# Windowed attention on one core: two adjacent rows per partition, or two blocks of 128 rows, in one transfer

## The chip, the core and the metric

The kernel runs on one core of a Trainium2 chip. The metric is the device time of one execution, in microseconds. Inputs and output lie in HBM, in float32.

## The reference

Queries, keys and values are `[4, 4096, 1536]`. The sequence is cut into windows of 64 rows, and attention is computed inside each window alone, over the full width of 1536:

```
q_w, k_w, v_w = x.reshape(B, S // 64, 64, D)          # B 4, S 4096, D 1536
logits = einsum('bnwd,bnud->bnwu', q_w, k_w) * D**-0.5
attn   = softmax(logits, axis=-1)
out    = einsum('bnwu,bnud->bnwd', attn, v_w)
```

Over the four batches there are 16,384 rows. The three inputs are 302 MB and the output is 100.7 MB.

## The kernel before

The rows of all batches are one list. `plan` (L25) cuts it into units: 63 body units of 256 rows, then two tail units of 128 rows. A unit has `G` blocks, and in each block a partition holds `R` adjacent rows; a unit is `128 * G * R` rows. The body has `BODY_G, BODY_R = 1, 2` (L40), the tail has `G = R = 1`.

`dram(x, u)` (L74) gives the view of HBM for a transfer: partition p, block g, and then R rows in one run. With R = 2 a partition's run is two adjacent rows, 12 KB of float32.

`load(u)` (L80) issues three transfers on GpSimd's queue (POOL, q0), for q, k and v; each casts to fp16 on the way (L84). There are four buffers of each, and loads are issued `PREFETCH = 3` units ahead, at the head of a unit's turn. The framework gives eight completion semaphores in rotation to POOL's transfers, so a ninth waits until the one eight before it has landed.

`scores(u, g)` (L116) transposes q and k of a block on TensorE against an identity (L140), eight 128x128 pieces to a PSUM tile `tp`, and evicts each tile into `xt`, in turn on VectorE (L145) and ScalarE (L147). The scores are accumulated over 12 chunks of the width in `lt`. With R = 1 the matmuls of a chunk follow its eviction by one tile, through `mm` (L126); with R = 2 all of them come behind the last transposes, in `finish_scores` (L165), and there each of the two row slots of k meets both row slots of q, so that one matmul has 256 columns.

`finish_scores` (L155) then takes exp on ScalarE (L177) for the blocks of the same window alone, and writes it into `et`, a constant tile whose other places were set to zero once. A window is 32 partitions wide with R = 2 and 64 wide with R = 1, so four or two instructions.

`values` (L180) multiplies `et` by ones for the row sums (L187), takes reciprocals on VectorE (L192), and multiplies `et` by v in pieces of 512 columns (L198). With R = 2 each piece is the sum of two matmuls, one for each row slot of v. The results are scaled by the reciprocal on the way out of PSUM, the first and third piece on ScalarE (L204), the second on VectorE (L206).

The program order is written out by hand (`tc.manual_schedule()`). In each turn come the loads of the unit three ahead; then for each block its scores and the values of the block before it; and the store of a unit behind its last values. Stores are issued on SP's queue (q1, L216), those of the last body units and of the first tail unit on POOL's queue behind the last loads. The last unit is stored in three pieces of 512 columns from SP (L208).

Of the kernel before, what the change touches and what calls it, by code (L numbers as in the profile page):

```python
# [36 lines left out]
    return units  # L37


BODY_G, BODY_R = 1, 2  # L40
PREFETCH = 3


# [218 lines left out]
```

## Time and profile before

| | |
|---|---|
| median of 3 runs | 958.6 us (958.33 to 958.67) |
| the profiled execution, its time and its span | 958.6 us, 956.8 us |
| granted TensorE clock, mean | 0.88 |
| body load, KB written, median us from issue to landing | 768 KB, 38.0 to 40.4 |
| body store on SP's queue, KB, median us from issue to landing | 1536 KB, 11.4 |
| packets on q0 (loads, four stores), on q1 (other stores) | 28,656, 9,072 |

The span is what the profile covers, from the first instruction to the last. Loads are counted in the profile by the bytes they write, which with the cast are half of those read. A page shows the busy time of each engine, then the span in 40 slices with the busy tenths of each, then the DMA queues, the chain of work that ended last, and groups of instructions. Waits name the waiting instruction first and what released it behind the arrow; the numbers are the sum in us, how often, and the longest.

### The profile page before, as it was taken

The page shows a single profiled execution, that of the slowest core. Times are in us where ns is not written, and L with a number is a line of the kernel's source. Part 1 is how long each engine was busy: PE and PEld are TensorE (multiplying, and loading weights), DVE is VectorE, ACT ScalarE, POOL GpSimd, SP SyncE. Part 2 cuts the span into 40 slices and gives each one's busy share as a digit, 9 for nine tenths or more (in the row PEclk, how much of TensorE's full clock was granted, in tenths as well). Part 3 has the DMA queues.
Part 4 walks back from the last instruction along what each step waited for, and adds up shares of the span by engine and source line. Part 5 has one row for each costly group of instructions (what it writes and reads, how often), then busy time and mean ns, then how long its engine had stood idle before and what let it go on. Part 6 is the DMA issues. An engine that isn't in the chain of part 4 may idle for free.

```text
span 956.8 us, 13110 instructions
## 1 busy us (share of the span) xinstructions
PE 658.4 (69%) x5624; PEld 482.7 (50%) x5624; DVE 240.6 (25%) x392; ACT 456.1 (48%) x705; POOL 105.8 (11%) x204
## 2 busy tenths in 40 slices
PE   4776766767767677676776766767667667676674
PEld 3454554645545555455464554555545445445452
DVE  1222222222222222222222222222222222222222
ACT  2544545444445454454545544445445444454445
POOL 3111011110110111101111011011110111111000
PEclk9978889888898898888978989889988999898888
DMA  9999999999999999999999999999999999999996
GB/s 185 242 268 263 275 269 258 279 258 269 270 256 279 257 270 279 250 277 267 259 280 255 271 272 255 279 259 269 279 252 275 266 261 279 257 269 273 253 252 268
DMA packets 37786, 252.51 MB, mean 264 GB/s; under 512 B 4192, under 2 KB 4192, under 8 KB 29664
## 3 DMA queue, kind: packets, MB, share of 16 engines
q0 software_dynamic: 28656, 156.51, 78.0%
q1 hardware_dynamic: 9072, 95.16, 24.0%
q8 instruction: 44, 0.72, 0.3%
q14 instruction: 14, 0.11, 0.0%
HBM read 301.99 MB, written 100.66 MB: 421 GB/s over the span
## 4 chain that ended last, share of the span: by engine, by line
DMA 86%; PE 8%; ACT 4%; issue 1%; DVE 0%; POOL 0%; ACTq 0%; POOLq 0%; DVEq 0%
DMA k<-in_k_dram 40%; DMA v<-in_v_dram 40%; DMA q<-in_q_dram 6%; PE tp L140 3%; PE lt L165 3%; ACT xt L147 2%; PE o L198 2%; ACT et L177 1%; ACT out_sb L204 1%; DVE xt L145 0%; PE lt L126 0%; PE sp L187 0%; POOL q L84 0%; ACTq L257 0%; POOL v L84 0%
## 5 line engine op out<-in xcount | busy, mean ns | idle before, releaser
L140 PE MATMUL tp<-ident,k 128*128 128x128 f16 x1536 | 259.6, 270 | 172.9 <-DMA k<-in_k_dram 172.9
L147 ACT COPY xt<-tp 128x1024 f16<-128x1024 f16 x192 | 194.3, 1012 | 348.3 <-PE tp L140 348.3
L140 PE MATMUL tp<-ident,q 128*128 128x128 f16 x1536 | 253.6, 264 | 52.1 <-ACT xt L147 21.4
L140 PEld LDWEIGHTS <-k 128*128 128x128 f16 x1536 | 156.8, 125 | 184.0 <-DMA k<-in_k_dram 183.8
L198 PE MATMUL o<-v,et 128*128 128x512 f16 x762 | 185.1, 378 | 61.5 <-ACT out_sb L204 61.4
L145 DVE COPY xt<-tp 128x1024 f16<-128x1024 f16 x192 | 132.7, 691 | 346.5 <-PE tp L140 346.5
L140 PEld LDWEIGHTS <-q 128*128 128x128 f16 x1536 | 163.0, 120 | 97.3 <-issue 67.6
L165 PE MATMUL lt<-xt 128*128 128x256 f16 x1512 | 188.4, 277 | 0.5
L204 ACT ACTIVATE out_sb<-o,rs 128x512 f32<-128x512 f32 x256 | 168.9, 686 | 19.0 <-PE o L198 11.1
L165 PEld LDWEIGHTS <-xt 128*128 128x128 f16 x1512 | 144.6, 100 | 31.2 <-ACT xt L147 13.8
L177 ACT ACTIVATE et<-lt,zeros 32x128 f16<-32x128 f32 (+1 forms) x256 | 91.8, 358 | 124.5 <-PE sp L187 114.6
L198 PEld LDWEIGHTS <-et 128*128 128x128 f16 x762 | 69.0, 96 | 146.9 <-issue 79.2
L206 DVE TENSOR_SCALAR out_sb<-o,rs 128x512 f32<-128x512 f32 x128 | 96.1, 750 | 151.4 <-PE o L198 151.4
L84 POOL DMA_DIRECT2D v<-in_v_dram x65 | 34.4, 529 | 343.1 <-PE o L198 309.9
L84 POOL DMA_DIRECT2D k<-in_k_dram x65 | 34.5, 531 | 332.4 <-DMA v<-in_v_dram 332.4
L192 DVE RECIPROCAL rs<-sp 128x2 f32<-128x2 f32 (+1 forms) x65 | 11.1, 170 | 209.1 <-PE sp L187 209.1
L84 POOL DMA_DIRECT2D q<-in_q_dram x65 | 34.6, 532 | 141.6 <-DMA k<-in_k_dram 140.8
L187 PEld LDWEIGHTS <-et 128*128 128x128 f16 x254 | 15.7, 97 | 1.9 <-ACT et L177 0.5
L187 PE MATMUL sp<-ones,et 128*128 128x1 f16 x254 | 15.6, 164 | 0.1
L216 POOL DMA_DIRECT2D out_dram<-out_sb x4 | 2.1, 532 | 25.2 <-ACT out_sb L204 22.3
L126 PE MATMUL lt<-xt 128*128 128x128 f16 x24 | 2.4, 221 | 2.6 <-ACT xt L147 1.7
L126 PEld LDWEIGHTS <-xt 128*128 128x128 f16 x24 | 1.4, 98 | 3.3 <-ACT xt L147 2.0
(10 smaller groups left out, 3.0 us busy)
## 6 DMA issues: line engine op xcount, KB each, us to landing
out_dram<-out_sb SPq DMA_DIRECT2D x60, 1536.0 KB, 11.4
q<-in_q_dram POOLq DMA_DIRECT2D x63, 768.0 KB, 40.4
k<-in_k_dram POOLq DMA_DIRECT2D x63, 768.0 KB, 38.1
v<-in_v_dram POOLq DMA_DIRECT2D x63, 768.0 KB, 38.0
out_dram<-out_sb POOLq DMA_DIRECT2D x3, 1536.0 KB, 9.1
q<-in_q_dram POOLq DMA_DIRECT2D x2, 384.0 KB, 30.3
k<-in_k_dram POOLq DMA_DIRECT2D x2, 384.0 KB, 26.2
v<-in_v_dram POOLq DMA_DIRECT2D x2, 384.0 KB, 21.9
```

What stands on the lines that cost most here:

```text
L84: nc.gpsimd.dma_start(out=dst, in_=dram(src, u))
L126: nc.tensor.matmul(lv[:, r, :, :], lhsT=xt[:, c, 1, r, :], rhs=xt[:, c, 0, :R, :], start=(c == 0), stop=(c == DC - 1),)
L140: nc.tensor.transpose(tp[:, c - c0, x, r, :], src[:, g * R + r, c * P : (c + 1) * P], ident)
L145: nc.vector.tensor_copy(out=dst, in_=tp)
L147: nc.scalar.copy(out=dst, in_=tp)
L165: nc.tensor.matmul(lv[:, r, :, :], lhsT=xt[:, c, 1, r, :], rhs=xt[:, c, 0, :R, :], start=(c == 0), stop=(c == DC - 1),)
L177: nc.scalar.activation(et[s, :, :, s], lv[s, :, :, s], EXP, bias=zeros[s], scale=scale)
L187: nc.tensor.matmul(sp[:, t, 0:1], lhsT=et[:, r, t, :], rhs=ones[:, 0:1], start=(r == 0), stop=(r == R - 1),)
L192: nc.vector.reciprocal(out=rs, in_=sp[:, :, 0])
L198: nc.tensor.matmul(o, lhsT=et[:, r, t, :], rhs=u.v[:, g * R + r, sl], start=(r == 0), stop=(r == R - 1),)
L204: nc.scalar.activation(dst, o, COPY, bias=0.0, scale=rs[:, t : t + 1])
L206: nc.vector.tensor_scalar_mul(dst, o, scalar1=rs[:, t : t + 1])
```

## The change

One line differs:

```
-BODY_G, BODY_R = 1, 2
+BODY_G, BODY_R = 2, 1
```

A body unit is still 256 rows, loaded in three transfers and stored in one. Now it has two blocks of 128 rows, and a partition holds one row of each: rows p and p + 128 of the unit in place of rows 2p and 2p + 1. A partition's run in HBM is one row, 6 KB, and there are two of them in a transfer, 768 KB apart. On the chip the tiles keep their size.

Each block takes the path of R = 1 that the tail units already had: scores through `mm` with 128 columns behind the transposes of the tile before, a window of 64 partitions in two exps, one reciprocal, and one matmul for each piece of the values. The two blocks of a unit follow one another, each with the values of the block before it between. The transposes and evictions keep their number and their shapes. The `et` tile is 128x128 in place of 2x2 of these. The tail units, the queues, the buffers and the prefetch depth are as they were.

## The prediction

> **What bounds the kernel now.** I read the page from the top: the span, the slices, the DMA queues, the chain. The profiled execution took 958.6 us (span 956.8, 1.8 around it), which is also the median of the runs, so terms worked out from the trace are added to 958.6.
>
> ```profile
> span 956.8 us, 13110 instructions
> PE 658.4 (69%) x5624; PEld 482.7 (50%) x5624; DVE 240.6 (25%) x392; ACT 456.1 (48%) x705; POOL 105.8 (11%) x204
> ...
> DMA  9999999999999999999999999999999999999996
> ...
> q0 software_dynamic: 28656, 156.51, 78.0%
> q1 hardware_dynamic: 9072, 95.16, 24.0%
> ...
> HBM read 301.99 MB, written 100.66 MB: 421 GB/s over the span
> ...
> DMA 86%; PE 8%; ACT 4%; issue 1%; DVE 0%; POOL 0%; ACTq 0%; POOLq 0%; DVEq 0%
> ```
>
> No compute engine is over 69%, while the 16 DMA engines are full in 39 slices of 40 and their waits are 86% of the chain. The two queues' shares sum to over 100%: a packet's recorded time overlaps the next one's, so its time is not what it occupies. The queue counts tell the packets: 65 x 3 loads x 128 partitions are 24,960, the four q0 stores 512, and 199 DMAs x 16 completion packets 3,184, together the 28,656 of q0. So today one packet is one partition's contiguous run: 12 KB read (6 KB written as fp16) for a body load, 12 KB for a body store.
>
> The waits say whether the loads ever come too late to keep the DMA engines full:
>
> ```profile
> POOL k L84 <- DMA v<-in_v_dram: 332.4, 62, 6.4
> POOL v L84 <- PE o L198: 309.9, 57, 6.8
> ...
> PE tp L140 <- DMA k<-in_k_dram: 172.9, 63, 4.4
> ```
>
> POOL waits for an older load to land (eight are in flight, 38 to 40 us from issue to landing), and PE waits 2.7 us per unit for k. The queue never runs dry and compute has slack: PE's idle time in the body costs nothing.
>
> The price of a smaller packet stands in the trace itself, because the two tail units already use R=1: 6 KB read per packet. One stretch with body loads alone, one with tail loads alone:
>
> ```profile
> DMA packets 535, 2.97 MB, mean 212 GB/s; under 512 B 52, under 2 KB 52, under 8 KB 535
> q0 software_dynamic: 535, 2.97, 103.6%
> ```
> ```profile
> DMA packets 374, 1.05 MB, mean 210 GB/s; under 512 B 46, under 2 KB 46, under 8 KB 373
> q0 software_dynamic: 373, 1.03, 105.4%
> ```
>
> The first is 4 to 18 us, the second 925 to 930 us. Written rate 212 against 210 GB/s: the smaller packets lose about 1%, but a window only counts this to a few packets. The packet records behind these lines are finer. A 12 KB load packet takes 474 ns and the next on its engine starts 19 ns before it ends: 455 ns each. A 6 KB one takes 248 ns with the same 19 ns: 229 ns. Two make 458 to 459, so 3.5 ns is the cost of one more load packet.
>
> **The change, part by part.**
>
> Transfers: bytes, DMA count, order and queues stay. Each partition's 12 KB becomes two runs of 6 KB, 768 KB apart in HBM. Per DMA engine, body loads go from 63 x 3 x 8 = 1,512 packets to 3,024. Cost: 1,512 x 3.5 ns = 5.3 us, all on the path because the DMA engines are the bound.
>
> Stores: 60 body stores on SP's queue, 480 packets per engine, become 960. A 12 KB store packet takes 460 ns behind another store and 473 ns behind a load (88% of the 7,680 records), each with 4 ns of overlap: 456 or 469. The 6 KB store at the very end takes 234 ns, half of 460 plus 4. So two in a row cost 460 against 456, and two that each follow a load cost 2 x (234 + 13 - 4) = 486 against 469. Loads and stores now take turns packet by packet; I expect this to go on with twice as many turns: 480 x (0.88 x 17 + 0.12 x 4) = 7.4 us. If two packets of a store go in a row, it is 480 x 4 = 1.9 us. No row here shows a store of two runs per partition, so both ends are kept; I take 7.4, since in the trace the turns change after every packet. The three 1.5 MB stores on POOL add 24 packets, 0.1 us. Below nothing I exclude: a shorter packet never moved bytes faster in these records. The upper end for loads is that a load which takes turns with a store also pays 13 ns: 480 x 13 = 6.2 us more.
>
> Descriptors: POOL's instruction is 532 ns and twice the runs may make it or the start longer. First issue at 1.26 us, first packet at 2.63: at most 1.4 us of making them is exposed, once. Between 0 and 1.4 us; I take 0.5. Later it is hidden by seven other loads in flight: even at 2.8 us for each of 195 loads POOL would be busy 546 us of 958. SP's store instruction (332 ns) is hidden behind idle SP time; if its packets came slower, loads would fill the engines meanwhile.
>
> Compute: scores of a unit go from 24 matmuls of 256 columns (277 ns each) to 24 of 128 (221 ns), values from 12 of 512 columns to 6, row sums from 4 to 2, exps from four of 359 ns to four of 310, reciprocals from 1 to 2 (170 ns, on a DVE that is 25% busy); the 48 transposes and 6 evictions stay, in two groups of three with scores behind each. In the body all this lies beside the DMA: the chain from k's landing to the next unit takes 12.0 us (923.35 to 935.35) of a period of 14.7 (the last two body k land at 908.64 and 923.35), and falls to about 10.2 by the tail below. POOL's v load waits for PE's values of the unit before; these come earlier, after the first half of the unit's scores, so nothing behind it on POOL (the next q, k, v) is late. The new wait of q and k loads on PE is for a buffer whose transposes ended a unit earlier.
>
> The tail is where compute shows:
>
> ```profile
> 884.70 38.60 DMA k<-in_k_dram
> 923.35 1.69 PE tp L140 x14
> 929.82 1.70 PE lt L165 x14
> 940.12 1.47 PE o L198 x6
> 946.30 1.84 ACT out_sb L204 x3
> ```
>
> These are the longest pieces of the chain from 919 us. The last body unit's k lands at 923.3; from there PE and ACT set the pace to 948.1, then the last stores run to 953.1. A half unit with R=1 is like tail unit N-2: its scores took 3.3 us (935.35 to 938.7), the last values of the kernel 1.8 (946.3 to 948.1), so the last body unit takes 2 x 5.1 = 10.2 instead of 12.0, and the values of that unit in the next step 1.8 instead of 2.9. That is 2.9 us of chain. The stores left at that time can use only what the DMA engines were idle for, about 2.4 us between 941 and 949 by the packet records. Gain 2.4, at least 0.
>
> The sum: 958.6 + 5.3 + 7.4 + 0.1 + 0.5 - 2.4 = 969.5; I say 969.
>
> The Trainium skill, "DMA: Bandwidth & Descriptors", Specifications, says that a transfer of 512 B or more already runs at line rate. By that the smaller packets would cost nothing and only the tail would count, some 956 us. The records speak against it: 2 x 229 is more than 455. The same page, Why small descriptors are slow, gives a fixed overhead of about 3 cycles per packet; at the 850 MHz of its Specifications that is 3.5 ns, an estimate which the load records bear out, and for 1,512 + 504 packets it would make 7.1 us and a time near 963.8. It has nothing of the 13 ns that a store behind a load shows here, and there I follow the trace.
>
> **Rivals.**
>
> Stores go two in a row (chance 0.2). The engines' turn would then come after both runs of a partition. For it: nothing in the trace; against it: every packet boundary is a turn now. 958.6 + 5.3 + 1.9 + 0.1 + 0.5 - 2.4 = 964.0.
>
> Packet size costs nothing and the tail decides (0.1 for faster by over 0.2%, the bound of what a measurement of this kernel can tell from no change, 1.9 us). Mechanism: less matmul work after the last body k, in the 24.8 us chain at the end. Price: -2.4 to -2.9, so 955.7 to 956.2. For it: the rates 212 and 210 differ by little more than the count of a window allows. It decides if a doubled packet costs below 0.25 ns on average over the 2,016 added per engine (1,512 + 504; 0.5 us of the 2.4). Between that and 1.9 us slower the result would be no change (0.05).
>
> Each added packet costs all of its recorded fixed time (0.05). Doubling 248 and taking off 474 gives 22 ns; 2,016 x 22 = 44 us, with the tail about 1001. Against it: shares over 100% show that 19 of the 22 lie beside the next packet. Something in between, such as 6 KB pieces 768 KB apart reading slower than the tail's adjacent ones, is in this case too.
>
> The change does not do what it says: it does; the loads become 128 x 2 x 1536 and the descriptors cannot be merged, since the two runs are not adjacent in HBM.
>
> **How the numbers follow.** Turns packet by packet 0.6, two in a row 0.2, the full fixed time or slower reads 0.05: slower 0.85. Same 0.05, faster 0.1. The likeliest case alone spans 967 to 972. The range reaches down to two in a row with the larger tail gain, no start cost and loads at 3 ns (2 x 229 - 455), 964.0 - 0.5 - 0.5 - 0.8, about 962, and up to loads that pay for turns too, a late start and no tail gain: 969.5 + 6.2 + 0.9 + 2.4 = 979.
>
> **What would show it.** DMA slices still full; q0 near 28,656 + 24,192 + 384 = 53,232 packets and q1 near 16,752; in load-only windows about 210 GB/s written; store packets at 247 ns with loads between them (in a row: 234); PE's wait for k longer than 2.7 us per unit, its busy time down; the tail from the last body k to the last ACT about 22 us instead of 24.8. I am wrong if load packets no longer start 19 ns before the last one ends, if slices in the body fall below 9 (descriptors or buffers late), or if POOL's load instructions grow to several us.

## The result, and the profile after

The changed kernel takes 969.1 us (median of 4 runs, 968.98 to 969.20) against 958.6: a ratio of 1.011, 95% interval 1.0092 to 1.0127. It is slower, by 10.5 us, at the forecast 969. The sum met the time; one of its terms was right for the wrong reason, and the experiments show which. The profiled execution took 969.0 us.

The page of the changed kernel, with the span, the engines, the DMA slices and the queues (packets, MB, share of the 16 engines' span):

```profile
span 967.2 us, 12600 instructions
PE 497.1 (51%) x5120; PEld 369.4 (38%) x5120; DVE 250.5 (26%) x453; ACT 429.9 (44%) x705; POOL 141.5 (15%) x204
...
DMA  9999999999999999999999999999999999999998
...
q0 software_dynamic: 53232, 156.51, 80.5%
q1 hardware_dynamic: 16752, 95.16, 24.8%
...
HBM read 301.99 MB, written 100.66 MB: 416 GB/s over the span
```

TensorE lost 161 us of busy time, and the kernel became slower: the DMA engines are full as before and move the same bytes at 416 in place of 421 GB/s. The packet counts are those foretold. The granted TensorE clock fell from 0.88 to 0.79; e3 below, with this compute at a clock of 0.80, is not slower than the kernel before, so the clock is not what costs. The waits of the changed kernel (sum in us, times, longest):

```profile
PE tp L140 <- DMA k<-in_k_dram: 244.0, 63, 7.0
...
POOL k L84 <- DMA v<-in_v_dram: 187.7, 45, 6.9
```

PE's wait for k went from 2.7 to 3.9 us per unit, 71 us in all: part of the compute that was saved became waiting for loads. The stretch from 4 to 18 us, loads alone:

```profile
DMA packets 1013, 2.96 MB, mean 212 GB/s; under 512 B 48, under 2 KB 48, under 8 KB 1013
q0 software_dynamic: 1013, 2.96, 107.7%
```

Twice the packets, the same 212 GB/s to within what a window can count, and a share that rose from 103.6 to 107.7%: more of each packet's time lies over its neighbour's. The packet records have load packets at 248 ns with 19 ns of overlap (229 each) and store packets at 247 ns in 94% of 15,360 and 234 in the rest.

Two views bear on the start and on the end. POOL's load instructions for q (busy us, mean ns), first of the kernel before, then of the changed one:

```profile
L84 POOL DMA_DIRECT2D q<-in_q_dram x65 | 34.6, 532 | 141.6 <-DMA k<-in_k_dram 140.8
```
```profile
L84 POOL DMA_DIRECT2D q<-in_q_dram x65 | 46.2, 711 | 303.8 <-DMA k<-in_k_dram 297.9
```

and the closing waits on SP, first of the kernel before, then of the changed one:

```profile
SPq L257 <- PEq L257: 3.1, 2, 2.6
SPq L257 <- DMA out_dram<-out_sb: 3.0, 3, 1.9
```
```profile
SPq L257 <- DMA out_dram<-out_sb: 5.8, 3, 5.0
SPq L257 <- PEq L257: 1.0, 2, 0.5
```

Before, SP waited 1.9 us for the last stores and then 2.6 us for the other engines; after, 5.0 for the stores and 0.5 for the engines. The last store landed 12.5 us later (953.4 to 965.9), but the span grew by 10.4 only.

For the experiments I use one more number from the packet records: the time from the first packet to the last, less what the 16 engines were idle on average (an engine counts as idle for each packet under 16 that is in flight). It is 946.8 us before and 959.5 after, 12.7 more. Here I call it the transfer time.

### The profile page after: what moved, and what is told of

Same layout as the page of the kernel before. It is cut to its first block, busy times and chain, and to the rows that moved or that the text cites. A ratio compares the mean times of both kernels' runs of the same rounds, so it can differ in the third digit from the quotient of the medians.

```text
span 967.2 us, 12600 instructions
## 1 busy us (share of the span) xinstructions
PE 497.1 (51%) x5120; PEld 369.4 (38%) x5120; DVE 250.5 (26%) x453; ACT 429.9 (44%) x705; POOL 141.5 (15%) x204
## 5 line engine op out<-in xcount | busy, mean ns | idle before, releaser
L140 PEld LDWEIGHTS <-k 128*128 128x128 f16 x1536 | 176.2, 116 | 270.6 <-DMA k<-in_k_dram 261.5
L126 PE MATMUL lt<-xt 128*128 128x128 f16 x1536 | 178.2, 249 | 171.7 <-ACT xt L147 136.9
L140 PEld LDWEIGHTS <-q 128*128 128x128 f16 x1536 | 176.5, 115 | 72.7 <-DMA q<-in_q_dram 57.4
L126 PEld LDWEIGHTS <-xt 128*128 128x128 f16 x1536 | 109.6, 110 | 224.3 <-ACT xt L147 159.0
L177 ACT ACTIVATE et<-lt,zeros 64x64 f16<-64x64 f32 x256 | 79.2, 309 | 148.4 <-PE sp L187 143.6
L198 PE MATMUL o<-v,et 128*128 128x512 f16 x384 | 116.9, 417 | 0.5 <-ACT out_sb L204 0.5
L84 POOL DMA_DIRECT2D q<-in_q_dram x65 | 46.2, 711 | 303.8 <-DMA k<-in_k_dram 297.9
L192 DVE RECIPROCAL rs<-sp 128x1 f32<-128x1 f32 x128 | 21.5, 168 | 223.7 <-PE sp L187 223.7
L84 POOL DMA_DIRECT2D v<-in_v_dram x65 | 46.1, 709 | 211.4 <-DMA q<-in_q_dram 177.4
L198 PEld LDWEIGHTS <-et 128*128 128x128 f16 x384 | 30.9, 104 | 19.6 <-issue 7.0
L187 PEld LDWEIGHTS <-et 128*128 128x128 f16 x128 | 14.1, 110 | 0.6 <-ACT et L177 0.6
L216 POOL DMA_DIRECT2D out_dram<-out_sb x4 | 2.7, 679 | 22.1 <-ACT out_sb L204 18.8
```

The costliest lines, as they stand in the source:

```text
L84: nc.gpsimd.dma_start(out=dst, in_=dram(src, u))
L126: nc.tensor.matmul(lv[:, r, :, :], lhsT=xt[:, c, 1, r, :], rhs=xt[:, c, 0, :R, :], start=(c == 0), stop=(c == DC - 1),)
L140: nc.tensor.transpose(tp[:, c - c0, x, r, :], src[:, g * R + r, c * P : (c + 1) * P], ident)
L177: nc.scalar.activation(et[s, :, :, s], lv[s, :, :, s], EXP, bias=zeros[s], scale=scale)
L187: nc.tensor.matmul(sp[:, t, 0:1], lhsT=et[:, r, t, :], rhs=ones[:, 0:1], start=(r == 0), stop=(r == R - 1),)
L192: nc.vector.reciprocal(out=rs, in_=sp[:, :, 0])
```

## The experiments

### Loads alone, stores alone, compute alone

Loads in two runs (e1), on the kernel before:

```
+    def rows_of(x, u):
+        return x[u.row0 : u.row0 + u.rows].rearrange("(a p) d -> p a d", p=P)
...
-            nc.gpsimd.dma_start(out=dst, in_=dram(src, u))
+            nc.gpsimd.dma_start(out=dst, in_=rows_of(src, u))     # dst is [P, 2, D]
```

> The kernel before (R = 2, its compute and its 12 KB stores) with only the body loads cut into two runs of 6 KB, rows p and p + 128 of the unit (so its windows hold other rows than the reference's). Theory (a load packet costs 3.5 ns beyond its bytes, a store packet pays 13 ns when it follows a load): 1,512 more load packets per engine are 5.3 us, the number of turns between loads and stores stays, a late start adds 0.5: 964.4 us. Rival A (a packet costs its whole recorded fixed time, 22 ns): 1,512 x 22 = 33 us, 992. Rival B (packets are free, the slower time of the changed kernel comes from its compute or its clock): 958.6.

Measured: 963.7 us (before in that call 958.9), ratio 1.0049 (1.0034 to 1.0064).

```profile
span 961.7 us, 13110 instructions
...
q0 software_dynamic: 52848, 156.51, 81.1%
q1 hardware_dynamic: 9072, 95.16, 24.0%
```

Transfer time 952.7, so 5.9 us for 1,512 packets per engine: 3.9 ns each. The number of turns did not quite stay: 450 store packets per engine follow a load in place of 425 (those that take 473 ns). At 13 ns that is 0.3 us, and without it a load packet costs 3.7 ns. Both rivals are out.

Stores in two runs (e2), the same view for `out` and L216:

> The kernel before with only the stores cut into two runs of 6 KB (output rows in another order than the reference's); loads stay at 12 KB. Theory (loads and stores take turns packet by packet): 7.4 us from SP's stores and 0.1 from POOL's: 966.1 us. Rival A (two packets of a store go in a row): 1.9 us, 960.6. Rival B (store packets are free): 958.6.

Measured: 965.0 us, ratio 1.0065 (1.0048 to 1.0082).

```profile
span 963.0 us, 13110 instructions
...
q0 software_dynamic: 29040, 156.51, 77.4%
q1 hardware_dynamic: 16752, 95.16, 24.9%
```

Transfer time 953.2, 6.4 us more, about 1 us under the sum, with 88% of the store packets at 247 ns. Loads and stores do take turns packet by packet; "two in a row" (960.6) is out.

The changed compute with 12 KB transfers (e3), on the changed kernel:

```
+    def run_of(x, u):
+        return x[u.row0 : u.row0 + u.rows].rearrange("(p a) d -> p (a d)", p=P)
...
-            nc.gpsimd.dma_start(out=dst, in_=dram(src, u))
+            nc.gpsimd.dma_start(out=dst, in_=run_of(src, u))      # stores likewise
```

> The changed kernel's compute (G = 2, R = 1) with the transfers of the kernel before: 12 KB per partition for loads and stores (rows 2p and 2p + 1 land in the two blocks, so its windows hold other rows than the reference's). Theory (the body is DMA, and the shorter chain behind the last body k brings the end forward): the last store is issued 2.9 us sooner; by the engines' idle time 2.4 can be had: 956.2 us, between 955.7 and 956.5. Rival A (the end hangs on transfers that are late for another reason, and the shorter chain brings nothing): 958.6.

Measured: 958.0 us, ratio 0.999 (0.998 to 0.9999).

```profile
span 955.9 us, 12600 instructions
PE 498.7 (52%) x5120; PEld 370.5 (39%) x5120; DVE 250.4 (26%) x453; ACT 429.7 (45%) x705; POOL 105.7 (11%) x204
```

The whole compute change, 160 us of TensorE, is worth 0.9 us, which the interval barely tells from nothing. That is not the 956.2 of the theory, and lies outside its 955.7 to 956.5. The chain did get shorter: the last scaling on ScalarE ended at 946.2 in place of 948.7, POOL issued its last store 3.0 us sooner. But the last store landed only 0.75 us sooner (952.7 against 953.4). In the kernel before the 16 completions of the last store lie 0.17 us apart; here 2.4 us. The first of them came 3.0 us sooner (950.3 against 953.3), the last 0.75: what the shorter chain gave, most DMA engines could use and the latest hardly.

The three parts add: 4.8 + 6.1 - 0.9 = 10.0, against 10.5 for the change.

### A larger dose of the load packets

The kernel before with loads in four runs of 3 KB (e4):

```
+    def halves_of(x, u):
+        flat = x[u.row0 : u.row0 + u.rows].rearrange("s d -> (s d)")
+        return flat.rearrange("(a p e) -> p a e", p=P, e=D // 2)
...
+                nc.gpsimd.dma_start(out=dst, in_=halves_of(src, u))   # body units alone
```

> The kernel before with the body loads cut into four runs of 3 KB, 384 KB apart (the inputs are shuffled within a unit, so its output is not the reference's). A dose of the same: theory (3.5 ns per load packet, whatever its size): 3 x 1,512 more packets are 15.9 us, a later start about 1: 975.5 us. Rival A (22 ns each): 100 us, 1058. Rival B (packets are free): 958.6. Rival C (shorter runs far apart also read slower in HBM): more than 980, and load packets that take longer than 113 + 22 = 135 ns.

Measured: 974.0 us, ratio 1.0156 (1.0141 to 1.0172).

```profile
span 971.5 us, 13110 instructions
...
q0 software_dynamic: 101232, 156.51, 87.2%
```

Load packets of 3 KB take 135 ns, as foretold, and the transfer time is 963.6: 16.8 us for 4,536 packets per engine, 3.7 ns each, or 3.6 without the 46 turns more per engine (0.6 us). From 12 KB to 3 KB, with runs 768 or 384 KB apart, the price goes by the packet. The packets' recorded time on q0 rises by some 100 us per engine (78.0% of 956.8 us to 87.2% of 971.5), which is the sum of Rival A, for a cost of 17: a queue's share cannot be read as time. The Trainium skill, "DMA: Bandwidth & Descriptors", Why small descriptors are slow, has about 3 cycles per packet (3.5 ns at the 850 MHz of its Specifications, an estimate); e1 and e4 bear that out with 3.7 and 3.6.

### Taking the turns away

Every body store on POOL's queue, behind the loads, in the kernel before (e5) and the changed one (e6):

```
-        eng = nc.gpsimd if i >= N - PREFETCH - 2 else nc.sync
+        eng = nc.gpsimd
```

> The kernel before with every body store issued on POOL's queue, so that loads and stores lie in one queue, a store's eight packets per engine behind one another, and no turns are taken. Theory (a store packet pays 13 ns when it follows a load packet of the other queue): 480 x 0.88 x 13 ns = 5.5 us less: 953.3 us, with store packets at 460 ns. Rival (the 13 ns belong to reads and writes being in flight together, or the loads behind a waiting store come late): 958.6 or slower, store packets still at 473 ns.

> The changed kernel with every body store on POOL's queue. Theory: 960 x 0.94 x 13 ns = 11.7 us less than 969.1: 957.4 us, store packets at 234 ns; what is left over e5 (953.3) is the bytes-free cost of 2,016 shorter packets, 5.3 + 1.9 us, less the shorter end. Rival (the turn is not what costs): 969.

Measured: e5 953.7 us, ratio 0.9947 (0.9929 to 0.9965); e6 959.3 us, ratio 1.0007 (0.9998 to 1.0017) to the kernel before. First e5, then e6:

```profile
span 951.9 us, 13105 instructions
...
q0 software_dynamic: 37296, 250.89, 101.9%
```
```profile
span 957.7 us, 12595 instructions
...
q0 software_dynamic: 69552, 250.89, 105.1%
```

With one queue, 87% of the 12 KB store packets take 460 ns, 93% of the 6 KB ones 234. Nearly all others take 13 ns more, 62 and 61 per engine: about one for each of the 63 stores on POOL's queue, the first of its packets, which comes behind a load of the same queue. So the 13 ns go with a store packet that follows a load, whichever queue the load is of. One queue makes such turns rare: 62 per engine in place of 425 in the kernel before, 61 in place of 904 in the changed one.

Transfer times are 942.4 and 949.2: 4.4 and 10.3 us less than with two queues. That is 12.1 ns for each of 363 turns, and 12.2 for each of 843. With most turns gone, what e6 is above e5 is 5.6 us, and 6.8 of transfer time, against 5.3 + 1.9 foretold for the shorter packets alone. The changed kernel is then level with the kernel before. e6 missed its 957.4 by 1.9 us: the 61 turns that stay are 0.8 of it, and 12.2 in place of 13 ns another 0.7.

### What holds the end

In the kernel before, the store of unit N-2 moved to SP's queue (e7), and the same in the changed kernel (e8):

```
+        eng = nc.gpsimd if N - PREFETCH - 2 <= i < N - 2 else nc.sync
```

> The kernel before with the store of the first tail unit (768 KB) on SP's queue in place of POOL's. In the profile of before POOL's closing drain ends 8.2 us behind its last issue, at 956.05, and 2.6 us after the last store has landed (953.4). Theory (the end hangs on POOL's drain, some 4 us behind the landing of POOL's last transfer): POOL's last transfer then is the store before (landed at 949.3, so drained by 953.3) and SP ends at 953.6: 2.3 us less, 956.3 us. Rival (the end hangs on the stores' landing alone): 958.6.

> The changed kernel with the first tail unit's store on SP's queue. In its profile POOL's drain ends at 966.45 and SP's last wait at 966.1, behind the last landing at 965.9. Theory (its end hangs on the last landing, which some DMA engines reach 2.9 us after the first, and no longer on the drain as in the kernel before): 0.3 us less, 968.8 us. Rival (the drain holds it as it held the kernel before): 2.6 us less, 966.5.

Measured: e7 956.0 us, ratio 0.9973 (0.9963 to 0.9983); e8 968.5, which is 9.7 us over the kernel before of its call, against 10.5. The closing waits on SP of e7:

```profile
SPq L257 <- DMA out_dram<-out_sb: 1.7, 3, 0.6
...
SPq L257 <- PEq L257: 0.7, 2, 0.5
```

The drain is the last long instruction on POOL, at L257; in the kernel before it starts at 947.8, takes 8.2 us (8217 ns) and ends at 956.05:

```profile
L257 POOLq DRAIN  x3: 46/102/8217, 947.8 to 956.6; - x3
```

In e7 the 2.6 us wait is gone with POOL's last transfer. The drain now ends at 953.2, 3.8 us behind POOL's last landing, as the theory has it, and the last store lands at 953.1. So the kernel before ended on POOL's closing drain, 2.6 us behind the last landing. The changed kernel ends on the landing, or within some 0.5 us of it: the drain ends at 966.45, the last landing is at 965.9, and e8 took off 0.6 us, not the 2.6 of the rival. In before, e2, e3, e7 and e9 the drain ended 3.8 to 4.1 us after POOL's last transfer had landed; in the changed kernel, e1, e4, e5, e6, e8 and e10 it was 1.3 to 2.0. The first group has at most 29,040 packets on q0, the second at least 37,152. Why the drain is shorter there is open.

### Why some DMA engines are late

The spread of the 16 completions of one transfer grows from a median of 1.5 us in the first 100 us to 8.0 between 800 and 900 us in the kernel before, and 7.1 in the changed one. Added instructions (e9), on the kernel before:

```
+        if i < N - 4:
+            for _ in range(80):
+                nc.gpsimd.memset(junk, 0.0)       # junk is [128, 1]
```

> The kernel before with 80 memsets of one column added on POOL in each of the first 61 turns (4,880 instructions; about 3 us of POOL per unit, which is 11% busy). The 16 completions of one transfer lie 1.5 us apart at the start and 7 to 10 us at the end: some DMA engines fall behind. Theory (the queue named instruction, 44 packets of 16 KB, falls on few engines, and these set the end): 4,880 instructions at 64 B are 19 more packets, so the spread grows by 0.4 of its 7 to 10 us and the time by about 3 us: 961.6. Rival (instruction packets are shared evenly, or the spread has another cause): under 0.8 us more (19 x 0.65 / 16), spread as before: 958.6 to 959.4.

Measured: 964.3 us, ratio 1.0058 (1.0042 to 1.0074), more than I expected.

```profile
span 962.3 us, 17990 instructions
...
q8 instruction: 44, 0.72, 0.3%
q14 instruction: 52, 0.43, 0.1%
```

The spread rose to a median of 15.3 us between 800 and 900 us, where the kernel before has 8.0, and the last store landed 5.6 us later. The 4,880 instructions came as 38 more packets of 8 KB on q14 (14 before) and none on q8. At 309 ns, the commonest time of such a packet, they are 11.7 us of one engine's time: shared evenly over 16 they would be 0.7 us, and half of the 11.7 showed in the time.

A rival is that POOL, now busy for 61% of the span, issued its loads too late. It is unlikely: between 100 and 900 us the DMA engines have no idle time in either kernel by the packet records, and the mean idle time that e9 has more, some 4 us, lies behind 920 us, when some engines have finished and others have not. So the added instructions make some DMA engines late, and the latest sets the end. That it is because the fetched packets fall on few engines fits the numbers and is not shown: the records do not name the engines, and no run adds work on POOL without instructions to fetch. Nor was it tried whether the 44 packets on q8 do the same in the kernel before. They are TensorE's program by their bytes: 0.72 MB are 64 B for each of its 11,248 instructions, and the changed kernel, with 1,008 of them fewer, has 40 packets. The Trainium skill, "DMA: Bandwidth & Descriptors", Latency and other measured facts, gives traffic of GpSimd's descriptor rings as its best guess for two slow engines; here the added memsets bring no descriptors, and the spread doubled all the same.

### A version that beats both

The kernel before with the body stores on POOL's queue and the first tail unit's store on SP's (e10):

```
+        eng = nc.gpsimd if i < N - 2 else nc.sync
```

> The kernel before with the body stores on POOL's queue (as e5) and the first tail unit's store on SP's (as e7). In e5 POOL's closing drain ended at 951.1, 0.9 us behind the last landing (950.2). Theory (the two gains add only as far as the drain leads): the end follows the last landing by about 0.9: 953.7 - 0.7 = 953.0 us. Rival (they add in full, 4.9 + 2.6): 951.1.

Measured: 952.9 us, ratio 0.9939 (0.9922 to 0.9955).

```profile
SPq L257 <- DMA out_dram<-out_sb: 7.2, 4, 5.4
SPq L257 <- PEq L257: 0.6, 2, 0.5
```

The end now hangs on the landing (950.1, POOL's drain 949.9, the end 951.0), and so the two gains do not add in full: 953.0 was foretold, 951.1 if they did.

## Why the prediction was right, and where it was not

**What bounds.** Right. With its transfers put back to 12 KB (e3) the compute change is worth under 1 us of 958, and with its transfers alone (e1 and e2) nearly the whole loss is there.

**Loads, 5.3 us.** Right: 5.9 in e1, of which 0.3 are turns, so 3.7 ns a packet where I took 3.5 from records that are read to 1 ns. In the span of e1 it shows as 4.9, because there too the drain at the end is 2.3 us shorter.

**Stores, 7.5 us.** Right in kind, a little large: 6.4 in e2, and e5 and e6 show by taking most turns away that they are what costs. The choice between the two ends of this term, turns packet by packet against two in a row, decided 5 us of the forecast, and "every packet boundary is a turn now" was the argument that held; of the shorter packets 94% follow a load, where I had carried over the 88% of the long ones. The 13 ns of the records came to 12.1 and 12.2 ns of transfer time for a turn taken away (e5, e6). In e2, with the 1.9 us of the packets taken off, it is (6.4 - 1.9) / 425, 10.6 ns for a turn added; the difference is open. Loads and stores of the change together made 12.7 us of transfer time against 12.8 in the sum, one a little over and the other a little under.

**Start, 0.5 us.** About 0.6. The first packet came 0.17 us later, and the engines were not full at once, because POOL takes 711 ns for a load in place of 532 and its first transfers are made one after another. The stretch from 2.6 to 4.6 us, with the DMA share in the column before the last, in the kernel before and the changed one:

```profile
2.60:4.60 2.00, 0.00 (x0) 0.00 (x0) 0.00 (x0) 0.00 (x0) 1.94 (x5) 1.00 1.01 144
```
```profile
2.60:4.60 2.00, 0.00 (x0) 0.00 (x0) 0.00 (x0) 0.00 (x0) 1.92 (x5) 1.00 0.68 106
```

That is 0.33 x 2 = 0.66 us, the 0.17 included. By the packet records the engines' mean idle time up to 10 us rose from 0.2 to 0.6 us, which with the 0.17 makes 0.6.

**The tail, -2.4 us.** This step failed, and its number came out by another way. The chain behind the last body k did shorten as worked out: from 923.35 to the last scaling's end at 948.72 before, from 936.07 to 958.51 after, 25.4 against 22.4 us.

```profile
936.07 0.29 PE L140 MATMUL tp<-ident,k 128*128 128x128 f16 x1 [3.44 <-DMA k<-in_k_dram]
...
956.09 2.42 ACT L204 ACTIVATE out_sb<-o,rs 128x512 f32<-128x512 f32 x4
```

But I let the stores fill 2.4 us in which the DMA engines were idle, and that was a mean over 16 of them. The latest engines were not idle; the last landing gained 0.75 us (e3). In the changed kernel the engines' mean idle time after 900 us is 2.7 us, where it was 3.4: 0.8 us less, the same. I also took the end of the span to follow the last landing at a fixed distance. In the kernel before it followed POOL's drain, 3.4 us after the landing; in the changed kernel it followed the landing by 1.3. With the measured terms, 12.7 + 0.6 - 0.8 - 2.1 = 10.4, the growth of the span. The -0.8 and the -2.1 together are near my -2.4, and that is luck: the second was in no term of the sum, and why the drain became shorter is open. Without it the kernel would have taken about 971.

**The rivals.** Free packets were to give about 956; e3, the same compute with the packets of the kernel before, took 958, since the tail is not worth what I gave it. The full 22 ns is out by e4, and two in a row by e2.

## What to carry to other kernels

Where the DMA engines are full, count packets before matmuls: one line that halved the contiguous run cost 1.1%, while 160 us less of TensorE were worth 0.1%. Price a packet by the distance from one start to the next, not by its recorded time, and count how often a store packet follows a load on the same engines; here, keeping loads and stores in one queue made that rare and brought 0.5% to the kernel before. A gain at the end of a kernel must be taken on the slowest DMA engine and on the last drain, not on the mean of the slices.

## What the runs showed of the hardware

- The next packet on an engine starts 19 ns before the recorded end of a load packet, and 4 ns before that of a store packet. Each further cut of a load's run costs 3.6 to 3.7 ns, from 12 to 6 and to 3 KB. A store packet behind a load packet takes 13 ns longer (473 against 460 at 12 KB, 247 against 234 at 6 KB), also where both lie in one queue (e5, e6), and costs 11 to 12 ns of transfer time.
- POOL takes 532 ns to issue a load of one run per partition, 711 with two and 745 with four. It shows in the time only at the start, with 0.6 us.
- POOL's closing drain ends 3.8 to 4.1 us after its last transfer has landed in five runs and 1.3 to 2.0 in seven, and it can set the end. The long drains are those with the fewest packets on POOL's queue (at most 29,040). The cause stays open.
- The 16 completions of one transfer fall apart by 7 to 8 us in the course of 950, and by 15 with 0.31 MB more of POOL's instructions, which cost 5.7 us.
